# One hybrid-decoder step: how the first products are fed, and where dense work stands around the second RWKV pair

## The chip, the cores and the metric

The kernel runs on one core of a Trainium2 chip. The metric is the device time in microseconds. Three runs of the kernel before took 1008.62, 1007.83 and 1004.70 us; the median is 1007.83 us. One more execution was profiled: its own time is 1006.88 us, and its span, from the first to the last instruction, is 1005.1 us.

## The reference, cut to what matters

One layer on 512 prompt tokens and 64 sample tokens (8 sequences of 8), all in fp32, with D = 1024. Tokens are kept as columns, so every activation is a tile of 128 channels by 576 tokens.

```
xn  = rmsnorm(x, g_mix)
P   = xn @ w_in                       # 14 RWKV columns of 128, q, k, v (4 heads each), 16 gate columns
Pr  = P[:, :14*128]; Pr += (shift(Pr) - Pr) * mu
o_a, S = rwkv7(Pr, S0)                # 8 heads of 64: S <- S*w + (S a) b^T + v k^T, y = S r, per token
o_b = diff_attention(q, k, v)         # prompt: causal; sample: 256 cached positions by page table
m   = sigmoid(gate_a) * (o_a @ w_br_a) + sigmoid(gate_b) * (o_b @ w_br_b)
x  += m @ w_out;  x += relu(rmsnorm(x) @ w_up)**2 @ w_down;  y = rmsnorm(x)
```

The RWKV recurrence is computed in chunks of 64 tokens. For each pair of heads a triangular system per chunk is solved, and then a chain over the 9 chunks carries the state.

## The kernel before, in words

**Dense products.** Every large product is split: a weight tile `raw` becomes `hi` (rounded, on ACT) and `lo = raw - hi` (on DVE), and the activation is `xh` and `xl` in the same way. A product of one 128 x 128 weight tile with half of the tokens (288 columns) is three matmuls: hi*xh, hi*xl, lo*xh. `stream` is a generator that yields before each of these matmuls, so a column of the input projection (8 k-tiles, two halves of the tokens) is 8 * 2 * 3 = 48 steps. `load` fetches a column in two pieces of four k-tiles on SP's queue.

**The start.** The first three columns (q, k and v of head 0) run together, k-tile by k-tile, in six PSUM banks (`qkv(0)`). Their weights come in pieces of four k-tiles, and x comes as eight tiles of 128 x 576, on SP's queue in the order x0, q, k, v (k-tiles 0 to 3), x1 to x3, q, k, v (4 to 7), x4 to x7. The small vector table `vec`, whose columns scale x into `xh` and `xl`, is fetched on ACT's queue, and behind it the table of constants `cst` (identity, masks, selectors). Nine matmuls of ones stand ahead of all others on TensorE.

**Order.** The kernel is written in one order, and a planner makes a fixed queue for each engine out of it: of the instructions that are ready by its own model, it takes the one with the lowest priority number first. Unmarked instructions are numbered as they are written, from zero upwards. `prio(FEED + ...)` gives large negative numbers (loads and splits of weights, the first x tiles), `prio(FILL + ...)` large positive ones. The planner knows nothing of TensorE's clock.

**Interleaving.** `waiting` is a list of dense generators. `take(n)` writes the next n dense matmuls at this place; they carry no tie, so the planner may also put them earlier where TensorE would be idle by its model. `fill(n)` writes them too, but inside `tc.issue_after(ring["mm"].ins)`: what the block issues on the engine of the given instruction is queued behind that instruction. Here that is the last matmul written, so these dense matmuls come behind it on TensorE. The tie holds for instructions of the given instruction's own engine only.

**RWKV.** `rwkv(hp)` is a generator for pair of heads hp = 0 to 3 and yields between its stages:
1. decay, norms and the A products: `pn`, `pw`, `pa`, `pk`, `pbn` and 36 `pA` matmuls, masked into ABR and ST by DVE;
2. transposes and states: `pV` (v transposed, into SVU), `pK` (keys transposed, into KBt), and `pI` (32 small matmuls of the old state s0, which an SP load brings);
3. the triangular solve: `pW` and `pZ` in four rounds, with nine dense matmuls tied behind each;
4. the new states of the sample tokens: masks `vm` on POOL (GpSimd), `pF`;
5. and 6. the output norm and `oa`.

`run(...)` advances the named pairs by one stage each, and `chain(pr)` runs the nine chunks of two pairs. In this text the first pair is hp = 0, the second hp = 1, and so on. In the order written out, the second pair's stages 1 and 2 follow each other, then come 106 loose dense matmuls, then its solve. In stages 1 and 2 of the pairs the dense groups are tied (`fill`) or loose (`take`) as the pair's number says.

The functions that the diff touches:

Of the kernel before, what the change touches and what calls it, by code (L numbers as in the profile page):

```python
# [8 lines left out]
F32 = mybir.dt.float32  # L9
F32R = mybir.dt.float32r  # L10
# [5 lines left out]
P = 128  # L16
D = 1024
KT = D // P
NPR = 512
NB = 8  # L20
NS = 64
NT = NPR + NS
NX = NT + NB
# [5 lines left out]
HALF = ((0, 288), (288, 288))  # L29
# [3 lines left out]
V_MU, V_W0, V_A0, V_KK, V_KA, V_RK, V_LW, V_LB, V_GM, V_GF, V_GO, V_SUB, V_END = (  # L33
    0, 14, 18, 22, 26, 30, 34, 38, 42, 50, 58, 66, 67)


C_ID, C_OB, C_M, C_MS, C_LM, C_I32, C_HS, C_SEL, C_MB, C_CM, C_END = (
    0, 128, 256, 384, 512, 672, 704, 706, 738, 746, 748)
# [3 lines left out]
def tile_hybrid_step(ctx, tc, xT, xsT, ktab, vtab, s0T, ptab, w_in, vecs, w2a2, g2, lamv,  # L42
                     w_bra, w_brb, w_out, w_up, w_down, cst, bias_p, bias_s,
                     yT, kTo, vTo, Sp, Ss, sh):
    nc = tc.nc
    PE, VE, AE, GE = nc.tensor, nc.vector, nc.scalar, nc.gpsimd
# [5 lines left out]
    def f32(ap):  # L52
        return ap.bitcast(F32)

    ring = {"job": 0}

    def act(out, in_, func=AF.Copy, **kw):
        ring["act"] = AE.activation(out=out, in_=in_, func=func, **kw)  # L58

    def tt(out, a, b, op, eng=None):  # L60
        ins = (eng or VE).tensor_tensor(out=out, in0=a, in1=b, op=op)  # L61
        if eng is None:
            ring["tt"] = ins

    def stt(out, a, s, b, op0, op1):
        VE.scalar_tensor_tensor(out=out, in0=a, scalar=s, in1=b, op0=op0, op1=op1)
# [16 lines left out]
    FEED, LATE, FILL = -1000000, 500000, 1000000  # L83

    @contextmanager
    def prio(at):
        was, tc.cur_priority = tc.cur_priority, at
        yield
        tc.cur_priority = was

    MUL, ADD, SUB, MAX = ALU.mult, ALU.add, ALU.subtract, ALU.max
# [18 lines left out]
    vec = const.tile([P, V_END], F32, name="vec")  # L110
    nc.scalar.dma_start(out=vec, in_=vecs)
    c = const.tile([P, C_END], F32, name="cst_sb")
    nc.scalar.dma_start(out=c, in_=cst)
    ident = c[:, C_ID:C_ID + P]
    onesblk = c[:, C_OB:C_OB + P]
    ones1 = const.tile([P, 1], F32, name="ones1")
# [17 lines left out]
    def v(i, n=1):  # L134
        return vec[:, i:i + n]
# [18 lines left out]
    def stream(src, kt, xh, xl, spans, evac, name, raws=None, together=False, banks=None,  # L154
               keep=None):


        his, los = [], []
        n = min(kt, ring["piece"])
        if src is None:  # L160

            job = ring["job"] = ring["job"] + 1
            raws = []
            his, los = ([t[:, k] for k in range(kt)] for t in keep)
        else:
            job, raws = raws or load(src, kt, name)

        def halve(i):
            raw = raws[i]
            with prio(FEED + 1000 * job + 100 if banks is None else FEED + 1001 + 40 * i + job):  # L170
                if keep:
                    hi, lo = (t[:, i * n:(i + 1) * n] for t in keep)
                elif banks is None or i == 0:
                    hi = ring["pool"].tile([P, n, P], F32R, tag="hi", name=f"hi_{name}_{i}")
                    lo = ring["pool"].tile([P, n, P], F32R, tag="lo", name=f"lo_{name}_{i}")
                else:
                    hi, lo = (zp.tile([P, NT], F32R, tag=f"Pt{job - 1}", name=f"{half}_{name}_{i}", bufs=2)[
                        :, :n * P].rearrange("p (k w) -> p k w", k=n) for half in ("hi", "lo"))
                act(hi, raw)
                tt(lo, raw, f32(hi), SUB)  # L180
                his.extend(hi[:, k] for k in range(n))
                los.extend(lo[:, k] for k in range(n))
        for i in range(len(raws)):
            halve(i)
        pss = banks or [psd.tile([P, 512], F32, tag="d", name=f"ps_{name}_{i}") for i in range(len(spans))]
        order = [(k, i) for i in range(len(spans)) for k in range(kt)]
        for k, i in sorted(order) if together else order:
            t0, w = spans[i]
            ps = pss[i]
            rh, rl = (x[k][:, t0:t0 + w] if isinstance(x, list) else x[:, k, t0:t0 + w] for x in (xh, xl))  # L190
            yield 1000 * job
            mm(ps[:, :w], his[k], rh, start=(k == 0), stop=False)
            yield 1000 * job
            mm(ps[:, :w], his[k], rl, start=False, stop=False)
            yield 1000 * job
            mm(ps[:, :w], los[k], rh, start=False, stop=(k == kt - 1))
            if k == kt - 1:
                with prio(FEED + 1000 * job + 200 + 20 * i):
                    evac(ps[:, :w], t0, w)
# [24 lines left out]
    def fill(n):  # L224

        with tc.issue_after(ring["mm"].ins):
            take(n)
# [31 lines left out]
    xh = xp.tile([P, KT, NX], F32R, name="xh")  # L259
    xl = xp.tile([P, KT, NX], F32R, name="xl")  # L260
# [7 lines left out]
    zw = pool("zw", 2, stack=ph1)  # L268
    gs = pool("gs", 2, stack=ph1)

    with tc.tile_pool(name="xin", bufs=2, reuse_waits="tile") as xin:
        xt = [xin.tile([P, NT], F32, name=f"x{k}", bufs=1) for k in range(KT)]
        xs_ = xin.tile([P, KT, NB], F32, name="xs", bufs=1)
        acc = xin.tile([P, NT], F32, name="acc", bufs=1)
        with prio(FEED):
            nc.sync.dma_start(out=xt[0], in_=xT[:, 0])
        first = [(j + 1, []) for j in range(3)]
        for k in range(0, KT, 4):
            for j in range(3):
                with prio(FEED + 1000 + 10 * k + j):  # L280
                    name = f"raw_{'qkv'[j]}0_{k}"
                    if k == 0:
                        raw = ring["pool"].tile([P, 4, P], F32, tag="raw", name=name, bufs=3)
                    else:
                        raw = zw.tile([P, 1 + NX], F32, tag="z" if j else "tz", name=name,
                                      bufs=2 if j else 1)[:, :4 * P].rearrange("p (k w) -> p k w", k=4)
                    ring["dma"] = nc.sync.dma_start(out=raw, in_=w_in[14 + 4 * j][:, k:k + 4])
                    first[j][1].append(raw)
            with prio(FEED + 1005 + 10 * k):
                for i in range(max(k, 1), k + 4):  # L290
                    nc.sync.dma_start(out=xt[i], in_=xT[:, i])
        ring["job"] = 3
        with prio(FEED + 4000):
            nc.sync.dma_start(out=xs_, in_=xsT)
        for k in range(KT):
            with prio(FEED + 1000 + 10 * k):
                act(xh[:, k, :NT], xt[k], scale=v(V_GM + k))
                stt(xl[:, k, :NT], xt[k], v(V_GM + k), f32(xh[:, k, :NT]), MUL, SUB)
        for k in range(KT):
            if k == 0:  # L300
                act(acc, xt[k], AF.Square)
            else:
                sq = xin.tile([P, NT], F32, name="sq")
                act(sq, xt[k], AF.Square)
                tt(acc, acc, sq, ADD)
        act(xh[:, :, NT:], xs_)
        tt(xl[:, :, NT:], xs_, f32(xh[:, :, NT:]), SUB)
        pst = tbank("pst1")
        with prio(FILL + 1155):
            colsum(pst, acc, ones1, 1)  # L310
# [354 lines left out]
    for h in range(HB):  # L665
        if h:
            qkv(h)
        for cc in range(2):
            GE.tensor_copy(
                out=qbd[64 * cc:64 * cc + 64, :, h, 8 * cc:8 * cc + 8],  # L670
# [51 lines left out]
    def m3(ap_, n):  # L722
        q, w = ap_.shape
        return ap_.rearrange("p (o w) -> p o w", o=1).broadcast_to([q, n, w])
# [17 lines left out]
    def rwkv(hp):  # L742
# [3 lines left out]
        r, k, vv = Pt[hp], Pt[4 + hp], Pt[8 + hp]  # L746
# [7 lines left out]
        pn = bank(f"pn{hp}")  # L754
        for t, o in enumerate(toks):
            mm(pn[:, 2 * t:2 * t + 2], sq[:, o:o + P], c[:, C_HS:C_HS + 2])
        (fill if hp != 2 else take)(8)
        nr = stat.tile([P, 10], F32, tag="nr", name=f"nr{hp}")
        ts(nr, pn[:, 0:10], 1e-24, MAX)
        GE.tensor_tensor(out=nr, in0=nr, in1=mhalf[:, :10], op=ALU.pow)  # L760
# [6 lines left out]
        for t0, n in HALF:  # L767
# [3 lines left out]
            pa = bank(f"pa{hp}{t0}")  # L771
            mm(pa[:, :n], al[:, hs], Pt[12][:, t0:t0 + n])
            act(aa[:, t0:t0 + n], pa[:, :n], AF.Tanh, scale=0.5, bias=hw0[:, 4 + hp:5 + hp])
        (fill if hp != 2 else take)(8)
        ts(u, u, 1.0, ADD)
        cum = tmp("cum")
        VE.tensor_tensor_scan(out=cum, data0=reset, data1=u, initial=0.0, op0=MUL, op1=ADD)
# [65 lines left out]
        for cs, pV in two_chunks(f"pV{hp}", vv):  # L843
            for a, c0, c1 in cs:
                src = pV[64 * a:64 * a + 64].rearrange("p (c w) -> p c w", w=P)[:, :(c1 - c0 + 1) // 2]
                act(SVU[64:128, c0:c1:2, 0], src[:, :, 0:64])
                act(SVU[0:64, c0:c1:2, 1], src[:, :, 64:128])
        if hp >= 2:
            fill(8)
        KBt = rb_.tile([P, NCH, 2, 64], F32, tag="KBt", name=f"KBt{hp}")  # L850
        for c0, cn in ((0, 4), (4, 4), (8, 1)):
# [5 lines left out]

        s0 = rt.tile([P, NB, 64], F32, tag="s0", name=f"s0_{hp}")
        nc.sync.dma_start(out=s0, in_=s0T[hp])
        (fill if hp == 3 else take)(8)  # L860
        pI = bank(f"pI{hp}")
        for b in range(NB):
            for par, rows in halves:
# [66 lines left out]
        vms = []  # L930
        for par in range(2):
            vm = rt.tile([P, NB, 64], F32, tag="G", bufs=3, name=f"vm{hp}{par}")
            tt(vm, m3(SVU[:, 8, par], NB),
               c[:, C_MB:C_MB + NB].rearrange("p (b o) -> p b o", o=1).broadcast_to([P, NB, 64]), MUL, GE)
            vms.append(vm)
        for par, rows in halves:
            mm(pF[rows], KBt[:, 8, par], vms[par].rearrange("p b i -> p (b i)"))
# [107 lines left out]
    def run(*stages):  # L1045
        for hp in stages:
            while Pt[8 + hp] is None:
                take(2)
            next(gens[hp], None)
# [3 lines left out]
    waiting += ga[:5]  # L1053
    run(0, 0)
    take(221)
    run(0, 1, 1)
    take(106)
    run(1)
    chain(0)
    run(2, 0, 1)  # L1060
    take(190)
# [422 lines left out]
```

## Time and profile before

| | |
|---|---|
| runs | 1008.62, 1007.83, 1004.70 us; median 1007.83 |
| profiled execution | 1006.88 us, span 1005.1 us |
| mean granted TensorE clock | 0.993 |
| TensorE matmul busy | 975.1 us, 97% of the span |
| weight loads on TensorE (beside the matmuls) | 919.4 us, 91% |
| DVE, ACT, POOL busy | 688.9, 497.0, 87.5 us |
| mean DMA rate | 105 GB/s |

In the page, PE is TensorE's matmuls and PEld its weight loads, which overlap them. A row of a timeline gives start, duration, engine, line, operation and tiles, how many instructions are merged, and in brackets how long the engine was idle before and what ended the wait. A row of the windows view gives, for one stretch of time, the busy time of each engine with its count of instructions, the granted TensorE clock as a share of full speed, the DMA share and the GB/s. Matmuls are pipelined, so the distance between two starts says more than a duration.

### The profile page before, as it was taken

How to read it: one execution, taken by the hardware profiler on the slowest of the kernel's cores; microseconds unless marked ns; L12 is line 12 of the kernel's file. 1: busy time of each engine (PE TensorE's matmuls, PEld its weight loads, DVE VectorE, ACT ScalarE, POOL GpSimd, SP SyncE). 2: the span in 40 equal slices, each digit the busy share in tenths (PEclk: the TensorE clock that was granted, in tenths of full speed). 3: DMA queues.
4: the chain of work that ended last, by engine and by line, in shares of the span. 5: the costliest groups of instructions: out<-in, count | busy, mean ns of one | idle time of the engine just before them, and what ended most of it. 6: DMA issues, size and time to landing. Idle time of an engine off the chain costs nothing.

```text
span 1005.1 us, 24415 instructions
## 1 busy us (share of the span) xinstructions
PE 975.1 (97%) x10012; PEld 919.4 (91%) x10012; DVE 688.9 (69%) x1459; ACT 497.0 (49%) x1094; POOL 87.5 (9%) x171
## 2 busy tenths in 40 slices
PE   9999999899999998999989999999999999999996
PEld 9999998898887887988779999999999999999996
DVE  6698566864946679444579898966666666666644
ACT  6576455354435355453334666644444444444732
POOL 2511001301010340000210000000000000000001
PEclk9999999999989999999999999999999999999999
DMA  7422673211111234323357642222222222221402
GB/s 266 136 70 83 205 223 114 61 64 45 43 59 45 69 106 152 104 81 113 103 182 225 206 140 86 83 95 85 88 92 85 85 84 85 84 87 41 135 3 95
DMA packets 50833, 105.75 MB, mean 105 GB/s; under 512 B 6066, under 2 KB 8114, under 8 KB 50594
## 3 DMA queue, kind: packets, MB, share of 16 engines
q1 hardware_dynamic: 47442, 96.95, 30.4%
q0 software_dynamic: 1648, 5.35, 1.5%
q8 instruction: 79, 1.29, 0.5%
q10 hardware_dynamic: 1632, 1.89, 0.5%
q14 instruction: 32, 0.26, 0.1%
HBM read 89.38 MB, written 14.78 MB: 104 GB/s over the span
## 4 chain that ended last, share of the span: by engine, by line
PE 83%; DVE 6%; ACT 4%; issue 3%; DMA 2%; POOL 1%; SPq 0%; DVEq 0%; ACTq 0%; POOLq 0%
PE ps_dn L72 20%; PE ps_g L72 8%; PE ps_z L72 8%; PE ua L1220 5%; PE ux L1220 5%; PE ps_wo L72 4%; PE ps_k L72 3%; PE uc L1220 3%; PE ub L1220 3%; PE ud L1220 2%; PE ps_bra L72 2%; PE ps_q L72 2%; PE pch L72 2%; PE ps_brb L72 2%; PE ps_v L72 2%
## 5 line engine op out<-in xcount | busy, mean ns | idle before, releaser
L72 PE MATMUL ps_dn<-q,hi_dn 128*128 128x288 f32 x768 | 154.7, 296 | 0.0
L72 PEld LDWEIGHTS ps_dn<-q,hi_dn 128*128 128x128 f32 x768 | 122.7, 188 | 1.4
L72 PE MATMUL ps_dn<-q,lo_dn 128*128 128x288 f32 x384 | 113.2, 295 | 0.0
L72 PE MATMUL ps_g<-xl,hi_g 128*128 128x288 f32 x256 | 79.7, 311 | 0.0
L72 PE MATMUL ps_g<-xh,hi_g 128*128 128x288 f32 x256 | 79.0, 309 | 0.0
L72 PE MATMUL ps_g<-xh,lo_g 128*128 128x288 f32 x256 | 79.0, 309 | 0.0
L72 PEld LDWEIGHTS ps_dn<-q,lo_dn 128*128 128x128 f32 x384 | 72.0, 188 | 0.0
L72 PE MATMUL ps_z<-xh,lo_z 128*128 128x288 f32 (+1 forms) x224 | 68.9, 308 | 0.0
L72 PE MATMUL ps_z<-xh,hi_z 128*128 128x288 f32 (+1 forms) x224 | 67.6, 302 | 0.0
L72 PE MATMUL ps_z<-xl,hi_z 128*128 128x288 f32 (+1 forms) x224 | 66.8, 298 | 0.0
L61 DVE TENSOR_TENSOR ya<-ya,ps_dn 128x288 f32<-128x288 f32 x96 | 43.2, 451 | 29.4 <-PE ps_dn L72 29.4
L58 ACT ACTIVATE hi_dn<-raw_dn 128x512 fp32r<-128x512 f32 x48 | 30.1, 628 | 57.0 <-PE ps_dn L72 57.0
L1220 PE MATMUL ua<-h_b,hi 128*128 128x288 f32 x256 | 53.2, 298 | 0.0
L1220 PE MATMUL ux<-h_t,hi 128*128 128x288 f32 x256 | 52.3, 296 | 0.0
L58 ACT ACTIVATE c<-c 128x288 f32<-128x288 f32 x112 | 48.4, 439 | 7.4 <-DVE c L61 5.8
L72 PEld LDWEIGHTS ps_g<-xh,hi_g 128*128 128x128 f32 x256 | 48.7, 190 | 3.1 <-issue 1.8
L72 PEld LDWEIGHTS ps_g<-xl,hi_g 128*128 128x128 f32 x256 | 48.6, 190 | 1.9
L72 PEld LDWEIGHTS ps_g<-xh,lo_g 128*128 128x128 f32 x256 | 48.6, 190 | 1.6 <-DVE lo_g L61 0.2
L58 ACT ACTIVATE hi<-a 128x1024 fp32r<-128x1024 f32 (+1 forms) x32 | 27.1, 846 | 42.0 <-PE ps_dn L72 34.2
L72 PE MATMUL ps_dn<-q,w 128*128 128x320 f32 (+1 forms) x336 | 46.3, 297 | 0.0
L61 DVE TENSOR_TENSOR lo<-s,hi 128x1024 fp32r<-128x1024 f32 x32 | 39.2, 1224 | 10.1 <-ACT hi L58 10.0
L72 PEld LDWEIGHTS ps_dn<-q,w 128*128 128x128 f32 x336 | 45.3, 190 | 0.1
(395 smaller groups left out, 2802.2 us busy)
## 6 DMA issues: line engine op xcount, KB each, us to landing
a<-in_w_up_dram SPq DMA_DIRECT2D x32, 512.0 KB, 3.4
raw_dn<-in_w_down_dram SPq DMA_DIRECT2D x64, 256.0 KB, 2.8
raw_g<-in_w_in_dram SPq DMA_DIRECT2D x32, 256.0 KB, 3.1
raw_z<-in_w_in_dram SPq DMA_DIRECT2D x28, 256.0 KB, 3.1
gt_d<-gg SPq DMA_DIRECT2D x16, 288.0 KB, 2.4
g<-gt_d SPq DMA_DIRECT2D x16, 288.0 KB, 3.6
kp<-in_ktab_dram SPq DMA_DIRECT2D x16, 256.0 KB, 4.5
vp<-in_vtab_dram SPq DMA_DIRECT2D x16, 256.0 KB, 3.8
```

The costliest lines, as they stand in the source:

```text
L58: ring["act"] = AE.activation(out=out, in_=in_, func=func, **kw)
L61: ins = (eng or VE).tensor_tensor(out=out, in0=a, in1=b, op=op)
L72: ring["mm"] = PE.matmul(out=out, lhsT=lhsT, rhs=rhs, start=start, stop=stop)
L1220: ring["mm"] = PE.matmul(out=ps[:, :288], lhsT=l[:, k], rhs=hb[blk][:, h, k], start=start and i == 0, stop=i == 11, skip_group_check=skip)
```

## The change

It has four parts.

- **Start.** x0 is fetched in two halves of 288 tokens, and `xh` and `xl` of k-tile 0 are made half by half. The first k-tile of q, k and v is fetched alone, on ACT's queue and with FEED's priority; k-tiles 1 to 3 follow on SP's queue behind x1. In `stream` the first split is of one k-tile, the second of three. The constants `cst` move from ACT's queue to SP's, behind x4 to x7.
- **Third pair (hp = 2), stage 1.** Its two groups of eight dense matmuls are tied (`fill`) where they were loose (`take`).
- **Second pair (hp = 1), stage 2.** A new tied group of eight stands between `pV` and `pK`, and the group between `pK` and `pI` is tied where it was loose. In the order written out, stage 2 now comes behind the 106 loose matmuls and directly ahead of the solve.
- **Masks.** The `vm` instructions of hp = 0 and 1 are written inside `issue_after(ring["tt"].ins)`, where `ring["tt"]` is the last tensor-tensor instruction on DVE.

```diff
     c = const.tile([P, C_END], F32, name="cst_sb")
-    nc.scalar.dma_start(out=c, in_=cst)
...
+        if banks:
+            four = [ring["pool"].tile([P, n, P], F32R, tag=half, name=f"{half}_{name}_0") for half in ("hi", "lo")]
...
+                elif i < 2:
+                    m = 3 if i else 1
+                    hi, lo = (t[:, i:i + m] for t in four)
...
+        raw0 = [ring["pool"].tile([P, 4, P], F32, tag="raw", name=f"raw_{'qkv'[j]}0_0", bufs=3) for j in range(3)]
         with prio(FEED):
-            nc.sync.dma_start(out=xt[0], in_=xT[:, 0])
...
+            for t0, n in HALF:
+                nc.sync.dma_start(out=xt[0][:, t0:t0 + n], in_=xT[:, 0, t0:t0 + n])
             for j in range(3):
...
+                nc.scalar.dma_start(out=raw0[j][:, 0:1], in_=w_in[14 + 4 * j][:, 0:1])
+                first[j][1].append(raw0[j][:, 0:1])
+        with prio(FEED + 1):
+            nc.sync.dma_start(out=xt[1], in_=xT[:, 1])
+            for j in range(3):
+                nc.sync.dma_start(out=raw0[j][:, 1:4], in_=w_in[14 + 4 * j][:, 1:4])
+                first[j][1].append(raw0[j][:, 1:4])
+            for i in (2, 3):
+                nc.sync.dma_start(out=xt[i], in_=xT[:, i])
...
+        with prio(FEED + 1045):
+            for i in range(4, KT):
+                nc.sync.dma_start(out=xt[i], in_=xT[:, i])
+
+            nc.sync.dma_start(out=c, in_=cst)
...
-                act(xh[:, k, :NT], xt[k], scale=v(V_GM + k))
-                stt(xl[:, k, :NT], xt[k], v(V_GM + k), f32(xh[:, k, :NT]), MUL, SUB)
+                for t0, n in HALF if k == 0 else ((0, NT),):
+                    t = slice(t0, t0 + n)
+                    act(xh[:, k, t], xt[k][:, t], scale=v(V_GM + k))
+                    stt(xl[:, k, t], xt[k][:, t], v(V_GM + k), f32(xh[:, k, t]), MUL, SUB)
...
-        (fill if hp != 2 else take)(8)
+        fill(8)
...
-        if hp >= 2:
+        if hp >= 1:
             fill(8)
...
-        (fill if hp == 3 else take)(8)
+        (fill if hp in (1, 3) else take)(8)
         pI = bank(f"pI{hp}")
...
+            with tc.issue_after(ring["tt"].ins) if hp < 2 else ExitStack():
+                tt(vm, m3(SVU[:, 8, par], NB),
+                   c[:, C_MB:C_MB + NB].rearrange("p (b o) -> p b o", o=1).broadcast_to([P, NB, 64]), MUL, GE)
...
     take(221)
-    run(0, 1, 1)
+    run(0, 1)
     take(106)
-    run(1)
+    run(1, 1)
     chain(0)
```

More of the change, by code (lines that the diff above doesn't have):

```diff
@@ L170, in halve @@
             with prio(FEED + 1000 * job + 100 if banks is None else FEED + 1001 + 40 * i + job):
+                m = n
                 if keep:
                     hi, lo = (t[:, i * n:(i + 1) * n] for t in keep)
-                elif banks is None or i == 0:
+                elif banks is None:
                     hi = ring["pool"].tile([P, n, P], F32R, tag="hi", name=f"hi_{name}_{i}")
                     lo = ring["pool"].tile([P, n, P], F32R, tag="lo", name=f"lo_{name}_{i}")
+                elif i < 2:
+                    m = 3 if i else 1
+                    hi, lo = (t[:, i:i + m] for t in four)
                 else:
@@ L180, in halve @@
                 tt(lo, raw, f32(hi), SUB)
-                his.extend(hi[:, k] for k in range(n))
-                los.extend(lo[:, k] for k in range(n))
+                his.extend(hi[:, k] for k in range(m))
+                los.extend(lo[:, k] for k in range(m))
         for i in range(len(raws)):
@@ L274, in tile_hybrid_step @@
         acc = xin.tile([P, NT], F32, name="acc", bufs=1)
+        first = [(j + 1, []) for j in range(3)]
+        raw0 = [ring["pool"].tile([P, 4, P], F32, tag="raw", name=f"raw_{'qkv'[j]}0_0", bufs=3) for j in range(3)]
         with prio(FEED):
-            nc.sync.dma_start(out=xt[0], in_=xT[:, 0])
-        first = [(j + 1, []) for j in range(3)]
-        for k in range(0, KT, 4):
+            for t0, n in HALF:
+                nc.sync.dma_start(out=xt[0][:, t0:t0 + n], in_=xT[:, 0, t0:t0 + n])
             for j in range(3):
[L280 to L291, printed above, removed]
+                nc.scalar.dma_start(out=raw0[j][:, 0:1], in_=w_in[14 + 4 * j][:, 0:1])
[7 more added lines that the diff above has]
+                nc.sync.dma_start(out=xt[i], in_=xT[:, i])
+        for j in range(3):
+            with prio(FEED + 1040 + j):
+                raw = zw.tile([P, 1 + NX], F32, tag="z" if j else "tz", name=f"raw_{'qkv'[j]}0_4",
+                              bufs=2 if j else 1)[:, :4 * P].rearrange("p (k w) -> p k w", k=4)
+                ring["dma"] = nc.sync.dma_start(out=raw, in_=w_in[14 + 4 * j][:, 4:8])
+                first[j][1].append(raw)
+        with prio(FEED + 1045):
+            for i in range(4, KT):
+                nc.sync.dma_start(out=xt[i], in_=xT[:, i])
+            nc.sync.dma_start(out=c, in_=cst)
         ring["job"] = 3
@@ L773, in rwkv @@
             act(aa[:, t0:t0 + n], pa[:, :n], AF.Tanh, scale=0.5, bias=hw0[:, 4 + hp:5 + hp])
-        (fill if hp != 2 else take)(8)
+        fill(8)
         ts(u, u, 1.0, ADD)
@@ L932, in rwkv @@
             vm = rt.tile([P, NB, 64], F32, tag="G", bufs=3, name=f"vm{hp}{par}")
-            tt(vm, m3(SVU[:, 8, par], NB),
-               c[:, C_MB:C_MB + NB].rearrange("p (b o) -> p b o", o=1).broadcast_to([P, NB, 64]), MUL, GE)
+            with tc.issue_after(ring["tt"].ins) if hp < 2 else ExitStack():
+                tt(vm, m3(SVU[:, 8, par], NB),
+                   c[:, C_MB:C_MB + NB].rearrange("p (b o) -> p b o", o=1).broadcast_to([P, NB, 64]), MUL, GE)
             vms.append(vm)
```

## The prediction

> **What bounds the kernel now.** I read the page first: TensorE (PE) is busy nearly throughout, so a change can win only its idle time, its slow time, or work.
>
> ```profile
> PE 975.1 (97%) x10012; PEld 919.4 (91%) x10012; DVE 688.9 (69%) x1459; ACT 497.0 (49%) x1094; POOL 87.5 (9%) x171
> ```
>
> Then the view of stretches, cut where the granted clock changes. Behind the label come the length, the busy time of PE, PEld, DVE, ACT and POOL with counts, and the clock as a share of full speed.
>
> ```profile
> 249.60:270.66 21.06, 20.40 (x153) 19.58 (x151) 20.53 (x39) 7.45 (x12) 0.10 (x1) 1.00 0.16 51
> 276.75:283.57 6.82, 6.82 (x120) 5.72 (x123) 2.50 (x7) 2.16 (x8) 2.67 (x2) 0.50 0.01 2
> 508.85:512.27 3.42, 1.56 (x8) 1.09 (x9) 1.75 (x4) 1.84 (x6) 1.59 (x1) 1.00 0.76 228
> 512.27:515.68 3.41, 3.41 (x14) 3.20 (x13) 3.10 (x6) 0.41 (x2) 0.21 (x1) 0.50 0.39 114
> ```
>
> Twice in mid-kernel the clock is halved: for 6.82 us from 276.75, in the second pair's stage 2 and what follows, and for 3.41 us from 512.27. What stands at the first place is in TensorE's timeline:
>
> ```profile
> 271.52 0.29 PE L72 MATMUL ps_g<-xh,hi_g 128*128 128x288 f32 x1
> ...
> 273.40 1.20 PE L76 MATMUL pK<-cst_sb,KB 128*128 128x128 f32 x9 [0.43 <-ACT SVU L58]
> 275.41 1.11 PE L72 MATMUL pI<-ST,s 64*64 64x16 f32 x32 [0.81 <-ACT KBt L58]
> 276.45 2.05 PE L72 MATMUL pn<-cst_sb,sq 128*128 128x2 f32 x10
> 278.36 1.31 PE L72 MATMUL pw<-P,wl 128*128 128x288 f32 x2
> 279.60 1.19 PE L72 MATMUL pW<-X,DM 32*32 32x32 f32 x72
> 280.72 0.61 PE L72 MATMUL ps_g<-xl,hi_g 128*128 128x288 f32 x1
> ...
> 283.17 0.97 PE L72 MATMUL pZ<-W,Y 32*32 32x32 f32 x72
> 284.07 0.40 PE L72 MATMUL ps_g<-xl,hi_g 128*128 128x288 f32 x1
> ...
> 285.46 0.82 PE L72 MATMUL pW<-X,DM 32*32 32x32 f32 x72
> ```
>
> Between 271.52 and 280.72, for 9.2 us, no dense matmul starts: there are transposes, small products and two waits. The loose dense work written ahead of this place was used up before it, and what follows in the list is tied behind `pW`. So the place pays for two waits and for the halved clock.
>
> **The second pair's stage 2.** Eight tied dense matmuls now follow `pV`, and eight follow `pK`. At full clock a dense matmul costs 14.49/111 = 0.131 us (second row below), so a group lasts 1.04:
>
> ```profile
> 6.12:10.51 4.39, 4.39 (x18) 4.37 (x19) 3.41 (x5) 3.83 (x7) 0.58 (x3) 1.00 0.99 357
> 10.51:25.00 14.49, 14.49 (x111) 14.49 (x110) 12.39 (x20) 10.20 (x18) 2.24 (x6) 1.00 0.79 260
> ```
>
> *Waits.* A group of 1.04 covers 0.43, the other 0.81: -1.24 us. Bounds: 0, if the planner's order puts the groups where nothing waits, and -1.24.
>
> *Clock.* Nine dense matmuls and what joins them took 2.45 us at half clock (280.72 to 283.17) and take 1.39 behind (284.07 to 285.46): 43% less. Of 6.82 us that is 2.95, which I take. Bounds: 3.41, if all of it scales with the clock, and 0, if the clock falls all the same. Would `pW` be ready sooner? It needs X, which DVE makes:
>
> ```profile
> 276.25 0.47 DVE L884 STREAM_TRANSPOSE X<-Y 128x288 f32<-128x288 f32 x1
> ```
>
> X is there at 276.7. In the new order `pI` ends at 276.5 - 1.24 + 2.09 for sixteen dense + 0.13 for one more that is tied behind it, so at 277.5. X holds nothing up, and `pn` and `pw` of the third pair, pulled forward here by the planner to fill a hole, need not stand here.
>
> *Cover.* The sixteen matmuls, 2.09 us, are missing elsewhere. As written before: 8 loose, 106 loose, solve; after: 106 loose, 8 tied, 8 tied, solve. So the loose stock ahead of `pV` is smaller by 8, and the list ends 8 sooner. At the first place DVE is busy 20.53 of 21.06 us and TensorE waits for it; at the second the next product waits for its input:
>
> ```profile
> 260.59 1.24 PE L72 MATMUL pbn<-rkp,cst_sb 128*128 128x288 f32 x4 [0.61 <-DVE rkp L66]
> ```
>
> ```profile
> 527.67 0.40 PE L72 MATMUL ps_bra<-oab,hi_bra 128*128 128x288 f32 x1 [0.69 <-DVE oab L61]
> ```
>
> Each gives back 0 to 1.04. DVE sets the pace at the first, so I take all of 1.04 there; at the second the input's own chain comes sooner too, and I take 0.
>
> *Moved.* The pair's copies on ACT and POOL and its load of s0 on SP now stand behind the 106 in the writing. The load is issued a hundred us ahead of `pI`, at a moment when SP's loads wait for their buffers. It costs nothing there; uncovered, the landing of some 4 us would still lie inside the 14 us of the 106.
>
> ```profile
> 173.69 0.90 SPq L859 DMA_DIRECT2D s<-in_s0T_dram  x2
> ```
>
> **The third pair's ties.** Their sixteen matmuls stand behind the first 72 of the solve in the list, and `pn` ran at 276: the tie is met before it matters. I take 0; where a group comes too late or fills a hole, 1.04 either way.
>
> **The masks.** `ring["tt"]` is an instruction of DVE, the masks run on POOL, and the tie holds only on the given instruction's own engine. So the edit ties nothing: 0. If it did, the one wait for a mask on record bounds it at 0.33 either way:
>
> ```profile
> 500.89 1.07 PE L72 MATMUL pF<-vm,KBt 128*64 128x512 f32 x2 [0.33 <-POOL vm L61]
> ```
>
> **The start.** The timeline's first rows, and two of the DMA view (the last number is the time from issue to landing):
>
> ```profile
> 0.74 0.41 ACTq L111 DMA_DIRECT2D vec<-in_vecs_dram  x1
> ...
> 1.12 4.21 PE L72 MATMUL warmup<-onesP 128*128 128x128 f32 x18 [1.12 <-DVE R L383]
> ...
> 1.24 0.41 ACTq L113 DMA_DIRECT2D cst_sb<-in_cst_dram  x1
> ...
> 4.23 0.78 ACT L58 ACTIVATE xh<-x,vec 128x576 fp32r<-128x576 f32 x1 [1.56 <-DMA vec<-in_vecs_dram]
> ...
> 6.12 0.85 PE L72 MATMUL ps_q<-xh,hi_q 128*128 128x288 f32 x2 [0.79 <-ACT hi_q L58]
> ...
> 10.67 1.01 SPq L150 DMA_DIRECT2D raw_q<-in_w_in_dram  x2
> ...
> 12.66 0.57 SPq L420 DMA_DIRECT2D wl<-in_w2a_dram  x1
> ```
>
> ```profile
> cst_sb<-in_cst_dram ACTq DMA_DIRECT2D x1, 374.0 KB, 4.4
> ...
> vec<-in_vecs_dram ACTq DMA_DIRECT2D x1, 33.5 KB, 3.5
> ```
>
> The first product waits for the split of q's four k-tiles; the small first pieces end that wait. What is late next? `vec`. The three new loads on ACT's queue carry FEED, `vec` carries none, and the planner puts FEED first: the loads at 10.67 were written after `wl` and went ahead of it. Then `vec` is issued at 0.74 + 3 * 0.50 = 2.24 (0.50 from 0.74 to 1.24), lands 3.5 later, at 5.74 instead of 4.23, and a half-wide `xh` of about 0.44 (an estimate: half of 0.78, and a little) lets the first product start at 6.2, as before. I take 0. Bounds: if `vec` keeps its place, the product starts behind the ones, at 1.12 + 4.21 = 5.33. 0.79 us at the first products' pace of 4.39/18 = 0.244 is 3.2 matmuls, worth 0.4; if the step from 0.244 to 0.131 comes one stretch of 3.41 us sooner as well, 1.6 more: -2.0. If `vec` queues 0.6 longer among more packets: +0.6. The three more splits and the second half of `xh` on ACT and DVE lie beside the 4.39 us of k-tile 0's products. `cst` goes past x4 to x7 and delays SP's later loads by 374 KB at 260 GB/s, 1.4 us; these feed columns whose products start behind the 25 us of the first three, so it costs nothing, and 1.4 uncovered.
>
> **Sum.** -2.95 - 1.24 + 1.04 = -3.2 against the profiled execution's 1006.88: **1003.7 us**. That execution lies 0.95 below the runs' median of 1007.83; against the median the forecast is -0.4%.
>
> **A rule weighed.** TensorE's rows ahead of the second fall of the clock:
>
> ```profile
> 509.61 0.77 PE L76 MATMUL pTy<-cst_sb,y 128*128 128x128 f32 x5 [1.18 <-DVE y L61]
> 510.21 0.65 PE L72 MATMUL pg<-P,wg 128*128 128x288 f32 x2
> 511.96 1.06 PE L72 MATMUL pg<-P,wg 128*128 128x288 f32 x2 [1.10 <-ACT oa L58]
> ```
>
> No wait is above 1.2 us, and the clock still fell. The Trainium skill (TensorE: Matmul & The Clock Gate, "Why this matters for your kernels") asks only that no idle gap exceed about 3 us. By that rule two groups of eight are enough, and the sum stands; by these rows they may not be, and it loses 2.95.
>
> **The rivals.**
> *The clock falls all the same.* A group is 1.04 of 3.41 us, 31%, beside transposes and small products, which did not hold the clock from 273 to 277. TensorE was busy for 46% of the stretch from 508.85, and that was too little. Against it: no wait is left here, and the longest stretch without dense work falls from 9.2 to some 2 (`pI` 1.1, `pW` 0.8). Time: 1006.88 - 1.24 + 1.04 = 1006.7.
> *`vec` keeps its place.* For it: no row shows two priorities on ACT's queue. Time: 1003.7 - 2.0 = 1001.7.
> *The cover runs out.* Where the second pair's A waits for DVE the loose stock ends early: all 2.09 us become idle, the clock falls there for a stretch as at 512.27 (3.41/2 = 1.7), and the old place keeps its half clock. 1006.88 - 1.24 + 2.09 + 1.7 = 1009.4, slower. It decides from ten missing matmuls on (1.24/0.131). Against it: `pbn` and `pA` keep TensorE at work there.
> *The edit does nothing* holds for the masks, at no price.
>
> **Chances.** Forecast 0.50 (own range 1002 to 1005.5), clock rival 0.22, start rival 0.13, slower rival 0.11, a reshuffled plan beyond these 0.04. Half a per cent, 5 us, is about what a measurement of this kernel can tell: faster is below 1002.8, slower above 1012.9. The forecast gives 0.19 of faster, since a median of runs can fall 0.9 off, the start rival 0.11, the others 0.02; slower are 0.05 of the slower rival and 0.02 of the reshuffle. So 0.32, 0.61 and 0.07. The range goes from 1000.0, the start rival with the other bounds of gain, to 1008.8, which leaves out the far part of the slower rival.
>
> **What would show it.** Clock 1.00 through the second pair's stage 2 and solve; `pK` and `pI` without waits and sixteen `ps_g` among them; waits for DVE at `pbn` or `pA` grown to some 1.6 together; `vec` issued fourth on ACT's queue and the first product near 6.2; the masks unmoved against POOL's memsets. Half clock in that stretch, a first product at 5.3, or waits above 2 us at the A products would prove me wrong.

## The result, and the profile after

The changed kernel takes 1011.1 us (median of 12 runs, 1007.08 to 1013.03) against 1005.25 for the kernel before (12 runs, 1002.43 to 1008.62): a ratio of **1.0051**, 95% interval 1.0037 to 1.0065. It is slower by some 5 us, and outside the range that was given. Its profiled execution has a span of 1010.2 us (1012.32 with what lies around it) against 1005.1, so that one pair of traces shows 5.1 us.

Where they went is read by laying the same instruction of the two traces side by side. The first product starts 2.48 us late, and from the first `pst` (27.32 against 30.17) to the first `pk` (182.32 against 185.19) all lies 2.86 late. Behind it the lag is 3.9. It grows to 4.7 at the second pair's `pbn`, falls to 3.4 and then 2.3 in the second pair's solve, is back at 4.2 ahead of the third pair's A, grows there by more than 3 again, and is 4.87 at the end.

**The start.** The changed kernel's timelines of ACT (with its DMA queue) and TensorE, as before: start, length, engine, line, operation, and in brackets the idle time ahead and what ended it.

```profile
0.74 0.41 ACTq L288 DMA_DIRECT2D raw_q<-in_w_in_dram  x1
...
4.05 0.31 ACT L58 ACTIVATE hi_q<-raw_q 128x128 fp32r<-128x128 f32 x1 [1.37 <-DMA raw_q<-in_w_in_dram]
4.05 0.35 ACTq L111 DMA_DIRECT2D vec<-in_vecs_dram  x1
...
8.01 2.96 ACT L58 ACTIVATE xh<-x,vec 128x288 fp32r<-128x288 f32 x5 [0.57 <-DMA vec<-in_vecs_dram]
```

```profile
1.12 4.21 PE L72 MATMUL warmup<-onesP 128*128 128x128 f32 x18 [1.12 <-DVE R L401]
8.60 0.61 PE L72 MATMUL ps_q<-xh,hi_q 128*128 128x288 f32 x1 [3.27 <-ACT xh L58]
```

`vec` is issued at 4.05, not at 0.74: in ACT's order it stands behind the split `hi_q`, and that waits for `raw_q` to land. `xh`, which needs `vec`, runs at 8.01 instead of 4.23.

**The third pair's A.** VectorE (DVE in the rows) and POOL of the changed kernel, and TensorE's product that waited:

```profile
348.25 3.87 DVE L61 TENSOR_TENSOR ST<-P,pe 64x576 f32<-64x576 f32 x1
```

```profile
346.32 2.16 POOL L836 MEMSET ST<- 64x1152 f32 x2
348.46 3.04 POOL L61 TENSOR_TENSOR vm<-SVU,cst_sb 128x512 f32<-128x512 f32 x3
```

```profile
354.37 1.24 PE L72 MATMUL pA<-ST,KB 128*128 128x128 f32 x8 [2.34 <-DVE ST L61]
```

A product of 64x576 (`r` times `pe`) that takes 0.75 us elsewhere took 3.87, 3.12 more, beside three masks of POOL that took 3.04 together. In the kernel before, the masks stood one memset later, and met the same product only at its end:

```profile
342.05 3.27 POOL L818 MEMSET ST<- 64x1152 f32 x3
345.41 3.55 POOL L61 TENSOR_TENSOR vm<-SVU,cst_sb 128x512 f32<-128x512 f32 x3
```

```profile
345.29 0.75 DVE L61 TENSOR_TENSOR ST<-P,pe 64x576 f32<-64x576 f32 x1
346.07 0.68 DVE L61 TENSOR_TENSOR ABR<-pA,cst_sb 64x512 f32<-64x512 f32 x1
```

There it was POOL that took longer, 3.55 for three masks in place of 3.04.

**The second pair's stage 2.** TensorE of the changed kernel. The waits of 0.43 ahead of `pK` and 0.81 ahead of `pI` are gone; two new ones, 0.21 and 0.46, stand ahead of `pV` and of a state product of the first pair (`pch`) that waits for `SVU`.

```profile
275.36 0.63 PE L76 MATMUL pV<-cst_sb,P 128*128 128x128 f32 x4 [0.21 <-DVE ST L61]
276.46 0.33 PE L72 MATMUL pch<-SVU,ST 128*64 128x64 f32 x2 [0.46 <-ACT SVU L58]
...
278.47 1.15 PE L76 MATMUL pK<-cst_sb,KB 128*128 128x128 f32 x9
...
280.82 1.11 PE L72 MATMUL pI<-ST,s 64*64 64x16 f32 x32
```

**The clock.** The stretches cut at the clock's edges (length; busy time of PE, PEld, DVE, ACT, POOL with counts; granted clock, DMA):

```profile
184.58:188.00 3.42, 2.81 (x12) 2.81 (x13) 1.66 (x5) 0.45 (x1) 3.08 (x9) 0.50 0.00 0
...
249.44:252.85 3.41, 3.41 (x11) 2.55 (x10) 1.06 (x2) 2.95 (x7) 2.46 (x6) 0.50 0.25 71
283.57:286.98 3.41, 3.41 (x87) 3.07 (x79) 0.54 (x3) 0.41 (x1) 2.67 (x2) 0.50 0.24 82
...
355.25:358.66 3.41, 3.41 (x18) 3.41 (x17) 2.61 (x6) 0.88 (x2) 0.00 (x0) 0.50 0.00 0
```

Between 15 and 990 us the clock is halved for four windows of 3.41 us, 13.65 in all, against 6.83 + 3.41 = 10.24 before. The one at 355.25 follows the wait of 2.34; the one at 512 is gone.

### The profile page after: what moved, and what is told of

Its sections match the earlier page's. It is cut to its first block, busy times and chain, and to the rows that moved or that the text cites. A ratio compares the mean times of both kernels' runs of the same rounds, so it can differ in the third digit from the quotient of the medians.

```text
span 1010.2 us, 24430 instructions
## 1 busy us (share of the span) xinstructions
PE 976.5 (97%) x10012; PEld 921.7 (91%) x10012; DVE 692.8 (69%) x1463; ACT 497.5 (49%) x1098; POOL 88.6 (9%) x171
## 3 DMA queue, kind: packets, MB, share of 16 engines
q8 instruction: 79, 1.29, 0.5%
## 4 chain that ended last, share of the span: by engine, by line
PE 82%; DVE 7%; ACT 3%; issue 3%; DMA 2%; POOL 2%; SPq 0%; DVEq 0%; POOLq 0%; ACTq 0%
PE ps_dn L72 20%; PE ps_z L72 8%; PE ps_g L72 8%; PE ua L1240 5%; PE ux L1240 5%; PE ps_wo L72 4%; PE ps_k L72 3%; PE uc L1240 3%; PE ub L1240 3%; PE ps_bra L72 2%; PE ud L1240 2%; PE ps_q L72 2%; PE pch L72 2%; PE ps_v L72 2%; PE ps_brb L72 2%
## 5 line engine op out<-in xcount | busy, mean ns | idle before, releaser
L58 ACT ACTIVATE hi<-a 128x1024 fp32r<-128x1024 f32 (+1 forms) x32 | 27.1, 846 | 42.1 <-PE ps_dn L72 34.3
```

## The experiments

Ratios are to the kernel before, with 95% intervals, from runs on the same chip; 0.001 is 1.0 us. Each experiment has its label in brackets; later on e5, say, stands for e5_masks_tied.

**The start alone** (e1_start: the kernel before with this, and nothing of the RWKV part):

```diff
-    nc.scalar.dma_start(out=c, in_=cst)
...
+            for t0, n in HALF:
+                nc.sync.dma_start(out=xt[0][:, t0:t0 + n], in_=xT[:, 0, t0:t0 + n])
+            for j in range(3):
+                nc.scalar.dma_start(out=raw0[j][:, 0:1], in_=w_in[14 + 4 * j][:, 0:1])
...
```

> The kernel before with the edit of the start alone. Theory: vec, issued at 4.05 us behind the split of q's first k-tile, makes the first product start at about 8.6 us and puts all that follows about 2.9 us later; at the first pk (182 before, 185 here) the wait of 2.66 us then falls into one window of the clock and not into two, and the clock is halved there for 3.4 us, 1.1 us more. So the start alone is 2.5 to 4.5 us slower than before (ratio 1.0025 to 1.0045), and the third pair's A stays free of long waits. Rival: a late start is taken up by waits further on, and what is lost is lost in the RWKV part; then this kernel stands within 1 us of the one before.

Measured **1.0026** (1.0012 to 1.0040). The first product starts at 8.87, behind the same two rows:

```profile
4.26 0.31 ACT L58 ACTIVATE hi_q<-raw_q 128x128 fp32r<-128x128 f32 x1 [1.58 <-DMA raw_q<-in_w_in_dram]
4.26 0.35 ACTq L111 DMA_DIRECT2D vec<-in_vecs_dram  x1
```

The third pair's A has no long wait here. Half of the loss is the start's. One detail of the expectation failed: the 2.67 us ahead of `pk` did not halve the clock in this execution, so the late start does not bring that window each time.

**`vec` first** (e3_vec_first). The changed kernel with

```diff
-    nc.scalar.dma_start(out=vec, in_=vecs)
+    with prio(FEED):
+        nc.scalar.dma_start(out=vec, in_=vecs)
```

> The changed kernel with the load of vec issued first on ACT's queue, ahead of the three single k-tiles. Theory: xh is no longer late, the first product starts between 5.3 and 6.2 us, the clock rises one window earlier or at the same 10.5 us as before, and the time falls by 2.9 to 5.5 us below that of the changed kernel, to a ratio of 1.000 to 1.002 against the one before: the RWKV part's loss stays. Rival: vec is not what is late (the halves of x or the small weight loads are), then the first product stays near 8 us and the ratio near 1.005.

Measured **1.0025** (1.0009 to 1.0042): 2.6 us better than the changed kernel, a little short of what was expected, and the first product starts at 7.09, not between 5.3 and 6.2. `vec` was what was late; what is late next is the second half of x's first k-tile. The planner issues the whole second k-tile between the halves, and on ACT the half's `xh` stands ahead of `hi_q`:

```profile
6.30 0.53 ACT L58 ACTIVATE xh<-x,vec 128x288 fp32r<-128x288 f32 x1 [2.13 <-DMA x<-in_xT_dram]
6.75 0.29 ACT L58 ACTIVATE hi_q<-raw_q 128x128 fp32r<-128x128 f32 x1
```

**`vec` first and the halves together** (e6_start2). Beside that:

```diff
-        with prio(FEED):
-            for t0, n in HALF:
+        for i, (t0, n) in enumerate(HALF):
+            with prio(FEED - 3 + i):
                 nc.sync.dma_start(out=xt[0][:, t0:t0 + n], in_=xT[:, 0, t0:t0 + n])
...
-            with prio(FEED + 1000 + 10 * k):
-                for t0, n in HALF if k == 0 else ((0, NT),):
+            for t0, n in HALF if k == 0 else ((0, NT),):
+                with prio(FEED + 1000 + 10 * k + (5 if k == 0 and t0 else 0)):
```

The last lines give the second half's `xh` and `xl` a priority number that is higher by 5, so that they come later.

> The changed kernel with vec's load first on ACT's queue and, on SP's, the two halves of x's first k-tile one behind the other (with vec first alone, the whole second k-tile was issued between them, and the second half landed at 6.30). Theory: now neither vec nor the second half is late; the first product starts at 5.3 to 5.8 us (7.09 with vec first alone), 1.3 to 1.8 us sooner, and the time is 0.5 to 2 us below that kernel's: ratio to before 1.0005 to 1.002. Rival: the landing is bound by the bytes that all queues want at once, so the first product stays near 7 and the ratio near 1.0025.

Measured **1.0031** (1.0017 to 1.0045): no better. The first product does start at 5.51, but k's first one waits, since its split is queued behind an `xh` that waits for the second k-tile:

```profile
5.51 0.40 PE L72 MATMUL ps_q<-xh,hi_q 128*128 128x288 f32 x1 [0.55 <-ACT hi_q L58]
...
7.32 0.40 PE L72 MATMUL ps_k<-xh,hi_k 128*128 128x288 f32 x1 [0.73 <-ACT hi_k L58]
```

The first attention product `pss` runs at 38.38 us here. It runs at 38.36 with `vec` first alone, and at 38.38 too in two executions with the start of before (r3_before and e8_pair2_masks, below). The 0.9 us by which the first product is sooner than in those two is lost behind it (in e9_both, below, which has the same start, `pss` runs at 37.83, 0.55 us sooner); the bytes that the first k-tiles need may set the pace, but that was not tried by itself.

**The second pair alone** (e4_second_pair: the kernel before with this):

```diff
-        if hp >= 2:
+        if hp >= 1:
             fill(8)
...
-        (fill if hp == 3 else take)(8)
+        (fill if hp in (1, 3) else take)(8)
...
-    run(0, 1, 1)
+    run(0, 1)
     take(106)
-    run(1)
+    run(1, 1)
```

> The kernel before with the second pair's groups of eight and the moved start of its stage 2 alone (nothing at the start, nothing in the third pair's preparation, nothing on the masks). Theory: the second pair's own stretch gains some 2.5 us, and the plan now puts three masks of POOL one memset earlier, at the same time as a product of VectorE on two operands in SBUF (r times pe); VectorE is blocked for the 3.1 us of the masks, the third pair's A waits 2.3 us and loses a further 1.7 us to the clock. Net 0 to +2 us (ratio 1.000 to 1.002). Rival: the clash comes from the third pair's groups; then this kernel is 2 to 3 us faster than before (ratio 0.997 to 0.998) and its third A waits for nothing long.

Measured **1.0017** (1.0006 to 1.0029). With no edit of the third pair and none of the masks, the clash is there, within 0.01 us:

```profile
343.63 3.88 DVE L61 TENSOR_TENSOR ST<-P,pe 64x576 f32<-64x576 f32 x1
```

```profile
343.84 3.04 POOL L61 TENSOR_TENSOR vm<-SVU,cst_sb 128x512 f32<-128x512 f32 x3
```

```profile
349.75 1.52 PE L72 MATMUL pA<-ST,KB 128*128 128x128 f32 x8 [2.35 <-DVE ST L61]
```

So moving sixteen dense matmuls in the plan also moved three masks on POOL, an engine that no line of this edit names. The rival, that the third pair's groups bring it, is out.

**The masks really tied behind A** (e5_masks_tied: the changed kernel, with a real dependency on POOL in place of the one that names an instruction of VectorE):

```diff
+        if hp == 2:
+            seen = stat.tile([P, 1], F32, tag="seen", name="seen")
+            ring["seen"] = GE.tensor_copy(out=seen, in_=ST[1][:, 8, 1, 63:64])
...
-            with tc.issue_after(ring["tt"].ins) if hp < 2 else ExitStack():
+            with tc.issue_after(ring["seen"].ins) if hp < 2 else ExitStack():
```

> The changed kernel with the masks of the first two pairs really held on POOL until VectorE has finished the third pair's A (a one-column copy on POOL that reads the last masked product, and the masks tied behind it). Theory: the product of VectorE that took 3.87 us takes 0.75, the wait of 2.34 us before the third pair's A and the halved clock behind it are gone, and the time falls by 3 to 4 us below that of the changed kernel (ratio to before 1.001 to 1.002); the late start stays. Rival: VectorE was late by its own work and the masks only coincide; then the wait and the time stay as they are (1.005), or the masks' later end delays the products that use them.

Measured **1.0038** (1.0024 to 1.0052). The product takes 0.75 us, the wait and the halved clock behind it are gone, but only 1.3 us of the expected 3 to 4 came: the masks, now at 357.21 for 4.69 us, fall on the next products of VectorE from SBUF, and `pF` waits 0.75 for them.

```profile
346.17 0.75 DVE L61 TENSOR_TENSOR ST<-P,pe 64x576 f32<-64x576 f32 x1
...
358.49 1.29 DVE L61 TENSOR_TENSOR DM<-DT,cst_sb 128x288 f32<-128x288 f32 x1
...
364.50 0.45 DVE L61 TENSOR_TENSOR DM<-DT,cst_sb 128x288 f32<-128x288 f32 x1
```

The same product takes 1.29 us beside the masks and 0.45 without.

**The masks tied behind `r` times `pe`**, ahead of A (e7_masks_st: the changed kernel; the tie as above, with the copy here):

```diff
             ST.append(st)
+            if hp == 2 and par:
+                seen = stat.tile([P, 1], F32, tag="seen", name="seen")
+                ring["seen"] = GE.tensor_copy(out=seen[rows], in_=st[rows, 8, 1, 63:64])
```

> The changed kernel with the masks of the first two pairs held on POOL only until VectorE's last r times pe of the third pair is done (a one-column copy of it on POOL, the masks tied behind), ahead of the third pair's A, not behind it: the place they had in the kernel before. Theory: that product takes 0.75 us, not 3.87, the third A waits for nothing long, and, other than with the masks behind the whole of A, pF does not wait for them and VectorE's next products on SBUF are not slowed; 3 to 4 us below the changed kernel, ratio 1.001 to 1.002. Rival: the products of VectorE that follow (masked A, out of PSUM) are blocked by the masks just as well, and the ratio stays at 1.004 to 1.005.

Measured **1.0015** (1.0002 to 1.0027), within what was expected: 3.6 us better than the changed kernel. That is the price of the clash; the two intervals together leave some 1.9 us either way.

**The second pair with the masks tied in this way** (e8_pair2_masks: the kernel before with the second pair's edit and this tie):

> The kernel before with the second pair's groups and its moved stage 2, and the masks held behind the third pair's r times pe in the same way; the start and the third pair's preparation as before. Theory: the second pair's gain of some 2.5 us is left without its price; ratio 0.997 to 0.9985. Rival: the gain of the second pair's stretch is taken back at waits behind it (the fourth pair's pbn and the solves, where the loose products are missing), and the ratio is 0.999 to 1.001.

Measured **0.9990** (0.9977 to 1.0004), which is where the rival had it, short of the gain that was expected. The masks now run beside VectorE's products out of PSUM, and these are not slowed (0.67 here; 0.67 too in e5_masks_tied, where no mask runs beside them):

```profile
345.17 3.05 POOL L61 TENSOR_TENSOR vm<-SVU,cst_sb 128x512 f32<-128x512 f32 x3
```

```profile
343.50 0.75 DVE L61 TENSOR_TENSOR ST<-P,pe 64x576 f32<-64x576 f32 x1
...
345.25 0.67 DVE L61 TENSOR_TENSOR ABR<-pA,cst_sb 64x512 f32<-64x512 f32 x1
```

Against the second pair alone that is 2.7 us; what is left of the second pair's own gain is 1.0 us, with an interval from a gain of 2.3 to a loss of 0.4. In this execution the clock is full through the whole of the second pair's stage 2 and solve, as forecast. But it is halved at three other places (the last row is the second pair's stretch):

```profile
182.02:185.43 3.41, 3.41 (x17) 3.41 (x16) 2.78 (x7) 1.02 (x2) 3.15 (x6) 0.50 0.00 0
366.34:369.75 3.41, 3.41 (x10) 2.59 (x9) 2.32 (x4) 2.07 (x4) 3.24 (x3) 0.50 0.30 102
509.70:513.11 3.41, 3.29 (x12) 3.00 (x12) 2.71 (x6) 0.51 (x3) 0.64 (x1) 0.50 0.51 153
270.00:292.00 22.00, 20.54 (x562) 18.48 (x561) 13.16 (x32) 9.61 (x26) 2.68 (x2) 1.00 0.12 41
```

**Both repairs** (e9_both: the changed kernel with the start of e6_start2 and the masks of e7_masks_st):

> The changed kernel with both repairs, the start of e6_start2 and the masks of e7_masks_st. Theory: the two losses are independent and add: 2.6 to 4.6 us from the start and 3 to 4 from the masks, below the changed kernel's 1.0051: ratio 0.996 to 0.9995. Rival: the clock's windows and the waits behind take a part back, and the ratio stays above 1.000.

Measured **0.9998** (0.9983 to 1.0014): the two repairs together take back all that the change had lost, 5.3 us, a little less than was expected. Against e8_pair2_masks this kernel has the third pair's ties and the new start; together they make no difference that can be seen.

**The kernel before, three times more.**

> The kernel before, unchanged, profiled once more, to see how far one profiled execution speaks for others. The prediction took 2.95 us of gain out of two windows of half clock in the second pair (276.75 to 283.57). Theory: the windows of 3.41 us in which the clock is set lie otherwise against the program in each execution, so the same code is halved in some of them for one window or none there, and the 2.66 us before the first pk halve the clock in some executions; the term was a draw, not a cost of the code. Rival: the same two windows are halved there each time, then the term is a property of the code.

> The kernel before, unchanged, a third profiled execution; theory and rival as for r1_before: under the theory the number of half windows between 270 and 290 us differs among the executions (0 to 2), and the first dense step to the full clock lies anywhere from 4 to 10.5 us; under the rival both are as in the first.

> The kernel before, unchanged, a fourth profiled execution; theory and rival as for r1_before.

In r2_before the windows lie as in the first execution, to 0.1 us (from 276.64 and 512.16). In the other two they lie otherwise; r1_before:

```profile
181.61:185.03 3.42, 3.42 (x16) 3.42 (x17) 2.42 (x6) 0.27 (x1) 3.14 (x8) 0.50 0.00 0
277.19:284.01 6.82, 6.82 (x95) 5.83 (x93) 2.62 (x7) 2.06 (x8) 2.67 (x2) 0.50 0.01 2
```

and r3_before:

```profile
244.52:247.93 3.41, 3.41 (x15) 2.67 (x9) 1.43 (x2) 3.10 (x7) 2.32 (x6) 0.50 0.09 13
278.65:282.07 3.42, 3.42 (x82) 3.23 (x81) 0.43 (x1) 1.12 (x3) 2.67 (x2) 0.50 0.02 5
384.47:387.88 3.41, 3.41 (x14) 3.06 (x12) 2.70 (x6) 0.96 (x2) 0.00 (x0) 0.50 0.79 267
```

From the clock records (us at half clock between 15 and 990, and of it from 270 to 292; us of TensorE's idle time up to its last matmul; when the clock first rises):

| execution | half clock | in the second pair | idle | first rise |
|---|---|---|---|---|
| before | 10.24 | 6.83 | 23.7 | 10.51 |
| r1_before | 10.24 | 6.83 | 24.0 | 4.12 |
| r2_before | 10.24 | 6.83 | 24.0 | 10.40 |
| r3_before | 10.24 | 3.41 | 24.5 | 5.59 |
| e1_start | 10.24 | 6.83 | 23.9 | 13.51 |
| after | 13.65 | 3.41 | 27.1 | 13.92 |
| e7_masks_st | 6.83 | 3.41 | 25.8 | 6.06 |
| e8_pair2_masks | 10.24 | 0.00 | 23.8 | 4.53 |
| e9_both | 6.83 | 0.00 | 21.2 | 7.16 |

Both theory and rival were half right. The old second pair does fall to half clock each time, for 6.83 us in four of five executions (e1_start has it too) and 3.41 in the fifth. In the five traces with its new form besides those in the table (e3, e4, e5, e6 and, below, e10), it is 3.41, 0, 0, 0 and 3.41. Its mean goes from 6.1 to 1.5 us. But over the whole kernel less than half of that is won: the sum is 10.24 in all five traces with the old form, and 8.2 on average in the five with the new form and without the clash (6.83 in e5, e7 and e9, 10.24 in e8 and e10). One place stands out: seven of the nine traces with the new form have a half window that starts between 363 and 373 us, and of the five with the old form only e1_start has one.

**More dense work ahead of the first `pk`** (e10_fill_pk: e8_pair2_masks with this):

```diff
-        (fill if hp != 2 else take)(8)
+        (fill if hp != 2 else take)(8 if hp else 24)
...
-    take(221)
+    take(205)
```

> The kernel of e8_pair2_masks with sixteen more dense matmuls written ahead of the first pair's pk, where TensorE waits 2.66 us for POOL in every kernel here, and sixteen fewer in the loose stock behind (205 for 221). Theory: the wait falls to some 0.6 us and the clock is no longer halved behind it: 2 to 3.5 us below that kernel, ratio to before 0.995 to 0.9975. Rival: what fills the wait is missing where the stock ends, and the ratio stays at 0.998 to 1.000.

Measured **0.9967** (0.9954 to 0.9980), 1002.96 us: faster than the kernel before by 3.3 us, some 8 us below the changed one, and 2.3 below e8_pair2_masks. The wait that every other kernel here has (2.65 to 2.67; e8_pair2_masks in the first row) is 0.48, and the clock behind it is full:

```profile
181.51 0.67 PE L76 MATMUL pk<-cst_sb,nb 128*128 128x128 f32 x4 [2.67 <-POOL nb L763]
```

```profile
181.64 0.66 PE L76 MATMUL pk<-cst_sb,nb 128*128 128x128 f32 x4 [0.48 <-POOL nb L763]
```

```profile
181.50:185.00 3.50, 3.36 (x26) 3.37 (x27) 3.50 (x9) 2.37 (x4) 3.16 (x9) 1.00 0.06 7
```

In the pair of traces the gain is the wait's: idle time falls from 23.8 us in e8_pair2_masks to 21.5. The sum of half clock stays at 10.24, since this execution is halved at three other places, one of them in the second pair:

```profile
278.26:281.67 3.41, 3.41 (x83) 3.07 (x82) 0.46 (x1) 0.05 (x1) 1.88 (x2) 0.50 0.12 44
363.59:367.00 3.41, 3.41 (x14) 3.27 (x15) 1.16 (x3) 1.72 (x3) 2.26 (x2) 0.50 0.07 26
380.66:384.07 3.41, 3.41 (x12) 2.85 (x12) 2.47 (x6) 0.44 (x1) 0.00 (x0) 0.50 0.43 103
```

## Why the prediction was wrong, step by step

- **The start, taken as 0 (bounds -2.0 and +0.6): measured +2.6.** That `vec` would stand fourth was right. The step that failed is "issued at 0.74 + 3 * 0.50 = 2.24". It counted what stands ahead on the DMA queue, not on the engine that issues: ACT works its list in order, the planner put the split `hi_q` ahead of `vec`, and that split waits for a landing (4.05). With `vec` first 2.6 us came back. `cst` moved past seven loads cost nothing that a trace shows, as said.
- **The masks.** That the edit does nothing was right: the changed kernel's lists of instructions with and without it are the same on all five engines. What failed is the sentence that the masks stay "unmoved against POOL's memsets". The second pair's edit moved them one memset ahead, onto a product of VectorE. Price: 3.6 us in the changed kernel (e7_masks_st), 2.7 in the second pair alone. The wait, 2.32 to 2.35, is in all four traces that have the second pair's edit and no mended masks (after, e3, e4, e6) and in no other; a halved window of 3.41 us right behind it is in two of them (after, e4). The case for it among mine was the "reshuffled plan", at 0.04. What could have been read: three masks at 345.41 and the product that ends at 346.04, side by side in the kernel before.
- **The waits of the second pair, -1.24.** `pK` and `pI` lost theirs, but 0.21 and 0.46 came ahead of `pV` and `pch`: -0.57 at the place. The two new waits stand ahead of the first group, which can't cover them. The longest stretch without a dense matmul fell from 9.2 us to 4.0 (273.36 to 277.32 in the changed kernel), not to the "some 2" of the prediction: no loose dense matmul is left beside `pV`.
- **The clock, -2.95.** At its place the mechanism held: 6.1 us of half clock on average before, 1.5 after, and 0.43 of 4.6 is 2.0. It was oversized by a third, and a gain at one place was taken for a gain of the kernel: over the whole kernel the mean falls by 2.0 us (10.24 to 8.2), worth some 0.9 by the same 0.43. In e8_pair2_masks, with no half clock in the second pair, the kernel still has 10.24 us of it, as all five executions with the old second pair have. Whether the order behind the second pair draws these windows to other places or they fell there by chance isn't settled by one trace for each kernel; the seven of nine against one of five between 363 and 373 us lean to the first.
- **The cover, +1.04.** It was not seen: `pbn`'s wait in the second pair is 0.6 in e8_pair2_masks as before, and idle time in all is 23.8 against 23.7 to 24.5.
- **The third pair's ties at 0** held as far as these intervals tell: e7_masks_st has 1.0015, which is what 1.0026 (the start alone) and 0.9990 (e8_pair2_masks) make without them.

The sum: +2.6 for the start, +3.6 for the masks, -1.0 for the second pair is +5.2; measured +5.1. Each term is known to 1.3 us or worse either way, so that they meet to 0.1 is luck. The forecast also counted from one execution (1006.88), 1.6 above the median of the twelve runs of before, which is small beside the miss. The rival "the cover runs out" named 1009.4, near the time, by a mechanism that is not there. As for the rule weighed ahead of the result: two groups of eight were enough at their place in five of nine traces, and in the other four the clock still fell for one window, with no wait above 0.5 us ahead of it in stage 2. So the absence of long waits was not enough there.

## What to carry to other kernels

When a load is added to an engine's queue, look at the engine's whole list: a load stands behind every instruction ahead of it that waits, not only behind loads (`vec` was issued at 4.05 us, not at 2.24). When a plan is rewritten, compare the order on the engines that the edit doesn't name, and see which operations of VectorE and POOL that both read SBUF come to lie side by side. Take a wait that is long in every trace (here 2.66 us at `pk`) before a clock window that differs from trace to trace.

## What the runs showed of the hardware

**VectorE and POOL shut each other out.** A product of two SBUF operands on VectorE took 3.87 and 3.88 us instead of 0.75 beside three POOL products of 3.04; the three took 3.55 where VectorE was there first; with one operand in PSUM VectorE took 0.67 beside the same masks, as it did without them; POOL's memsets, which read nothing (three in 3.27 us from 342.05 in the kernel before), left the same product at 0.74. The Trainium skill says just this (SBUF — State Buffer, "Who interferes with whom"): a VectorE instruction with two SBUF inputs contends with a GpSimd instruction that reads SBUF and not with one that only writes, and the shared port is an exclusive lock. These rows agree. The blocked product came through only behind the third mask: it ended at 352.12, the masks at 351.50. The record of starts doesn't show who held the port: the blocked product's start is 0.21 us ahead of the first mask's, and in the kernel before a product with a start 0.12 ahead was not blocked.

**The clock's windows are not tied to the program.** Their edges lie on a grid of 3.41 us whose offset differs between executions of one kernel: the first rise came at 10.51, 4.12, 10.40 and 5.59 us in four executions of before, whose `pss` stands at 39.31, 38.46, 39.41 and 38.38. The Trainium skill (TensorE: Matmul & The Clock Gate, "What's actually happening") calls the window free-running and the cold start run-variable; the rows agree. It also ties the fall to idle windows, and here they do not agree: the clock fell at 249.44 in the changed kernel behind a window in which TensorE was busy throughout,

```profile
246.02:249.44 3.42, 3.42 (x73) 3.17 (x66) 0.45 (x2) 2.42 (x6) 1.59 (x1) 1.00 0.31 81
```

of which some 1.4 us were dense products, and the rest products on 32x32 tiles (`pWc`, `pC`) and of two columns (`pn`). The ends of matmuls are modelled in these rows. What kind of work counts as activity these runs do not settle.
